# Projection pairs with a fourth PSUM bank, a fixed place for the S5 scan, and weights of merge and output gate cast ahead

## The chip, the cores and the metric

The kernel runs on one core of a Trainium2 chip. The measure is the device time of one execution in microseconds (us). The core has five engines with a queue each: TensorE (PE; matmuls and transposes into PSUM), VectorE (DVE), ScalarE (ACT), GpSimd (POOL) and SyncE (SP, which here only issues DMA transfers). An engine takes its instructions in the order of its queue, so one that waits for a semaphore holds all that stand behind it.

## What is computed

One layer of an encoder: 2048 tokens of width 1024, in float32. The input is normalised, one wide product makes all the projections, four branches (an S5 state-space scan, chunkwise retention, differential attention, cross-attention to 256 memory tokens) are gated each, projected and merged, and one output product is added to the input. Cut to what bears on the change:

```python
h = rms_norm(x, norm_g)
proj = einsum('bsd,dc->bsc', h, w_in)      # 12 pieces of 512 columns, merge: 4 x 1024
ssm_u, ssm_gate, ..., mem_q, mem_gate, merge = split(proj)
# S5: complex diagonal scan over tokens, 32 groups of 16 channels, 64 states each
z = gelu(y + d_skip * u)
a_out = z * sigmoid(z @ w_glu + b_glu) * silu(ssm_gate)      # the output gate (GLU)
branches = stack([a_out, b_out, c_out, m_out])               # S5, retention, differential, memory
br = einsum('bsnc,ncd->bsnd', branches, w_branch)
merged = sum(sigmoid(merge + b_merge) * br, axis=branches)
x = x + merged @ w_out
```

## The kernel before

The tokens are worked in two blocks of 1024 (block 0, block 1). Each block runs through retention, differential attention (with the S5 input u at its tail), **projections** (about 690 to 1183 us in block 0, 2264 to 2750 in block 1), and **merge_output** (to 1460 and 3030), whose output stage ends the block. Every float32 product is made of three passes over operands that are split into a high and a low part: high x high, high x low, low x high. A high part is a cast on ScalarE (names that end in h), a low part the difference, on POOL for weights (L1264 p_l, L460 w1l) and on VectorE for data (br_l, zl, x_t2l). One 128x128 by 128x512 pass is one matmul; twelve of them, four slices of the contraction times three passes, make what is called a product below.

**Projections.** A `Pair` makes 256 columns of w_in for all 1024 tokens by seven products instead of eight (Strassen's scheme): operands t1 to t4 are sums of slices of the activations, mixed on VectorE by `x_mix` at the start, and sums of the weight's quarters a11, a12, a21, a22 are made in `prepare` (L1274 to L1286) from the raw tiles p_r. `product(s)` runs them, in the order 11, t2, t1, t3, 21, 22, t4, into three PSUM banks a, b, c (a from the pool mm, b and c from sc), and `collect(s)` adds what is in a bank to the tiles p_t: L1311 after t2, L1313 and L1314 after t3, L1320 after 22, L1323 after t4. L1314 reads bank c (t1), into which 22 is then written. There are 21 such pairs in a block, behind a first pair that is made in the plain way by `proj_tr`, between the steps of x_mix.

Beside the products, 16 **S5 scans** run in each block (`s5_scan`), one for every eight products: eight small matmuls into a bank of sc (L993), then on VectorE L998 to L1010, one multiply on POOL (L1011), s_x on VectorE (L1014 to L1017), eight more matmuls (L1021, L1023), then a GELU, and z goes to DRAM.

**merge_output.** 32 units (branch n, 128 output columns d), each two times twelve matmuls with a weight of w_branch (w1h, w1l, from a raw tile w_r) and the branch's split output (br_h, br_l), into banks of sc; VectorE multiplies by the gate mg_g (L1238), POOL adds up (L1239). Eight heads and halves of memory attention (`Mem`; m_q, m_kv) are woven into the first 114 of the merge's 128 steps. Then s5b is opened: z is loaded (L1045), split into zh and zl (L1048, L1050), and the **output gate** `s5_glu` runs its products (w_glu, bank mm) between the merge's last steps.

The program is a list of instructions in the order in which the source emits them; a scheduler, at build time, then orders them anew for each engine, so that an instruction may stand ahead of others that come before it in the source. The order of each engine is fixed from then on.

## Time and profile before

| | us |
|---|---|
| three executions, median (lowest, highest) | 3105.1 (3104.0, 3107.03) |
| the profiled execution | 3110.96 |
| its span in the profile | 3109.2 |
| TensorE busy in the span | 2931.0 (94%) |
| VectorE, ScalarE, POOL busy | 1927.7, 1336.3, 1280.6 |

The times in the views are microseconds from the start of the span. A list of waits gives an engine's idle time ahead of a line, by what released it. The chain of waits goes back from the end of a window, at each step to what released it. A window's row gives the busy time and the number of instructions of each engine, and the clock that TensorE was granted, as a share of its higher level.

### The profile page before, as it was taken

What the parts mean: (1) busy time and instruction counts of PE and PEld (TensorE: products, weight loads), DVE (VectorE), ACT (ScalarE), POOL (GpSimd) and SP (SyncE); (2) the same over time, 40 slices, a digit from 0 to 9 for tenths busy, and PEclk for the clock granted to TensorE, in tenths of its full rate; (3) what the DMA queues carried; (4) which work ended last, traced back from release to release, by engine and by line L of the source; (5) the groups of instructions that cost most, each with busy time, mean ns of one, the idle gap of its engine ahead of it and who ended that gap; (6) DMA issues with size and microseconds to landing.
All of it is one profiled execution on the core that took longest, in us unless ns stands there. A gap on an engine that the chain in (4) does not pass through costs nothing.

```text
span 3109.2 us, 43566 instructions
## 1 busy us (share of the span) xinstructions
PE 2931.0 (94%) x14514; PEld 2398.1 (77%) x14514; DVE 1927.7 (62%) x4581; ACT 1336.3 (43%) x3357; POOL 1280.6 (41%) x1189
## 2 busy tenths in 40 slices
PE   5999999998999999989999999999999999999899
PEld 4777777777877877777788878878878878777677
DVE  5885577757655545656543378888776545446654
ACT  3323355553333344423433257776733333344322
POOL 2543543324444543566132242233154444434660
PEclk9999999999999999999999999999999999999999
DMA  5332422133443426555521120121144344355553
GB/s 151 99 90 76 129 72 66 60 91 123 141 137 127 134 102 199 178 179 177 160 73 43 61 64 25 55 60 31 36 139 137 131 138 139 109 175 169 191 159 99
DMA packets 319343, 351.77 MB, mean 113 GB/s; under 512 B 28479, under 2 KB 238478, under 8 KB 319118
## 3 DMA queue, kind: packets, MB, share of 16 engines
q1 hardware_dynamic: 314734, 340.59, 34.9%
q0 software_dynamic: 2304, 8.39, 0.9%
q8 instruction: 115, 1.88, 0.3%
q14 instruction: 110, 0.90, 0.1%
q10 hardware_dynamic: 2080, 0.01, 0.0%
HBM read 247.98 MB, written 100.93 MB: 112 GB/s over the span
## 4 chain that ended last, share of the span: by engine, by line
PE 68%; DVE 12%; POOL 7%; issue 5%; DMA 4%; ACT 3%; SPq 1%; POOLq 0%; DVEq 0%; ACTq 0%
PE sc L1302 17%; PE mm L74 8%; PE mm L76 8%; PE mm L75 8%; PE mm L1302 6%; PE o L806 3%; PE sc L74 3%; PE sc L76 3%; PE sc L75 3%; POOL rms_r L138 2%; PE tr L797 1%; PE sc L752 1%; PE sc L751 1%; POOL mg L1239 1%; DMA w_r<-in_w_in 1%
## 5 line engine op out<-in xcount | busy, mean ns | idle before, releaser
L1264 POOL TENSOR_TENSOR p_l<-p_r,p_h 128x512 fp32r<-128x512 f32 x260 | 364.1, 1402 | 427.8 <-ACT p_h L1263 397.9
L74 PE MATMUL mm<-w5h,xh 128*128 128x512 f32 x1024 | 438.5, 428 | 16.9 <-ACT xh L577 15.6
L75 PE MATMUL mm<-w5l,xh 128*128 128x512 f32 x1024 | 408.2, 399 | 2.9 <-DVE w5l L443 2.9
L76 PE MATMUL mm<-w5h,xl 128*128 128x512 f32 x1024 | 408.9, 399 | 0.0
L138 POOL TENSOR_TENSOR rms_r<-rms_m,mhalf 128x1 f32<-128x1 f32 (+1 forms) x228 | 177.8, 781 | 506.3 <-DVE rms_m L136 437.3
L1263 ACT CAST p_h<-p_r 128x512 fp32r<-128x512 f32 x260 | 160.3, 620 | 345.4 <-DVE p_r L1277 82.5
L758 ACT ACTIVATE pr<-sc,nm 128x512 f32<-128x512 f32 (+3 forms) x320 | 200.1, 626 | 147.0 <-DVE nm L756 145.1
L74 PEld LDWEIGHTS mm<-w5h,xh 128*128 128x128 f32 x1024 | 196.9, 192 | 47.2 <-ACT xh L577 16.0
L76 PEld LDWEIGHTS mm<-w5h,xl 128*128 128x128 f32 x1024 | 195.2, 191 | 44.4
L75 PEld LDWEIGHTS mm<-w5l,xh 128*128 128x128 f32 x1024 | 197.0, 192 | 31.8 <-DVE w5l L443 3.3
L74 PE MATMUL sc<-br_h,w1h 128*128 128x512 f32 x512 | 208.8, 408 | 10.0 <-ACT w1h L459 5.8
L75 PE MATMUL sc<-br_l,w1h 128*128 128x512 f32 x512 | 205.1, 400 | 7.3 <-DVE br_l L1188 7.3
L76 PE MATMUL sc<-br_h,w1l 128*128 128x512 f32 x512 | 205.1, 401 | 0.5 <-POOL w1l L460 0.5
L756 DVE TENSOR_REDUCE nm<-sc 128x1 f32<-128x512 f32 (+3 forms) x320 | 193.3, 605 | 9.1 <-PE sc L752 5.0
L1239 POOL TENSOR_TENSOR mg<-mg,mg_g 128x512 f32<-128x512 f32 x96 | 146.2, 1526 | 96.0 <-DVE mg_g L1238 87.9
L806 PEld LDWEIGHTS o<-vt,at 128*128 128x128 f32 x1088 | 141.8, 192 | 40.5 <-ACT at L799 32.5
L806 PE MATMUL o<-vt,at 128*128 128x128 f32 x1088 | 152.1, 279 | 19.1 <-ACT at L799 18.9
L460 POOL TENSOR_TENSOR w1l<-w_r,w1h 128x512 fp32r<-128x512 f32 x88 | 122.9, 1410 | 98.5 <-ACT w1h L459 89.2
L1302 PE MATMUL sc<-xh,p_h 128*128 128x512 f32 x336 | 138.7, 413 | 22.9 <-DVE p_t L1314 22.3
L443 POOL TENSOR_TENSOR w5l<-w_r,w5h 128x512 fp32r<-128x512 f32 x72 | 97.8, 1360 | 110.2 <-ACT w5h L442 93.3
L1302 PE MATMUL mm<-xh,p_h 128*128 128x512 f32 x336 | 133.4, 397 | 4.4 <-ACT p_t L1309 4.4
L1302 PE MATMUL sc<-xl,p_h 128*128 128x512 f32 x336 | 135.4, 403 | 0.0
(388 smaller groups left out, 7690.5 us busy)
## 6 DMA issues: line engine op xcount, KB each, us to landing
p_r<-in_w_in SPq DMA_DIRECT2D x88, 512.0 KB
w_r<-in_w_in SPq DMA_DIRECT2D x144, 256.0 KB
me_d<-p_t SPq DMA_DIRECT2D x128, 256.0 KB
mg_g<-me_d SPq DMA_DIRECT2D x64, 512.0 KB
s_m<-mats_d SPq DMA_DIRECT2D x32, 640.0 KB
w_r<-br SPq DMA_DIRECT2D x64, 256.0 KB
w_r<-in_w_branch SPq DMA_DIRECT2D x64, 256.0 KB
n_x<-in_x SPq DMA_DIRECT2D x16, 512.0 KB
```

Of the source, the lines that this page charges most:

```text
L74: PE.matmul(out, l[0], r[0], start=first, stop=False)
L75: PE.matmul(out, l[0], r[1], start=False, stop=False)
L76: PE.matmul(out, l[1], r[0], start=False, stop=last)
L138: G.tensor_tensor(r, m, mhalf[:, 0:n], op=ALU.pow)
L460: G.tensor_tensor(lo, raw, hi.bitcast(F32), op=ALU.subtract)
L756: V.tensor_reduce(nm, s[:, 0:n], axis=AX.X, op=ALU.max, negate=True)
L758: A.activation(e[:, 0:n], s[:, 0:n], AF.Exp, bias=nm, accum_out=self.zz[:, m, c:c + 1])
L806: PE.matmul(self.o[:, 0:128], self.at[c][:, q * 128:(q + 1) * 128], self.st["vts"][c][:, q, :], start=c == 0 and q == 0, stop=c * 4 + q == ...
L1239: G.tensor_tensor(dst, dst, t, op=ALU.add)
L1263: A.copy(hi, x)
L1264: G.tensor_tensor(lo, x, hi.bitcast(F32), op=ALU.subtract)
L1302: PE.matmul(o, l[:, k, :], r, start=first and k == 0 and q == 0, stop=k == 3 and q == 2, skip_group_check=True)
```

## The change

- **Pair**: the products come as 11, t2, t1, t3, 21, t4, 22; t4 gets a bank d of its own (pool tr), so that 22 writes bank c one product later. The sums in `collect` follow. The raw tiles p_r come from two pools of two in turn, and the first pair's are loaded in the tail of differential attention.
- **S5 scan**: a scan takes seven products instead of eight, its parts at fixed places behind the products 7j + 1, 7 to 11 and 13; it uses the bank o; the multiply of L1011 goes from POOL to VectorE (32 instructions).
- **Start of the projections**: all four steps of `x_mix` run ahead of each of the first pair's products, and t4 is split ahead of t1.
- **Merge**: the first unit's weight has a pool of its own (w0h, w0l) and is loaded and cast while the last pairs run, with three of the four tiles of the first branch; the rings of w1h and w1l for w_in are four deep instead of six.
- **Output gate**: the split of z is spread in eighths over the merge's steps 4 to 18 behind memory attention, the weights of w_glu are loaded one ahead, and the gate's products begin at step 20 instead of 18.

In the order of the instructions it shows at three places. VectorE, projections of block 0, around the scan whose end stands ahead of L1313 and L1314 (p_t are the collected sums, s_ tiles the scan's, p_s and p_r sums of the weight's quarters). Before:

```order
L1277 TENSOR_TENSOR p_r<-p_s,p_r 128x4x128
L1002 TENSOR_TENSOR s_w<-s_p_11398,s_p_11399 128x128
L1003 TENSOR_TENSOR s_w<-s_p_11398,s_p_11399 128x128
L1007 SCALAR_TENSOR_TENSOR s_y<-rho,carry,s_w 128x128 x2
L1274 TENSOR_TENSOR p_s<-p_r 128x512
L1010 TENSOR_TENSOR s_q_11425<-s_y,s_m 128x256
L1276 TENSOR_TENSOR p_r<-p_r 128x4x128
L1015 TENSOR_TENSOR s_x<-s_q_11425,s_q_11426 128x128
L1016 TENSOR_TENSOR s_x<-s_q_11426,s_q_11425 128x128
L1017 COPY carry<-s_x 128x2
L1313 TENSOR_TENSOR p_t<-sc,p_t 128x512
L1314 TENSOR_TENSOR p_t<-sc,p_t 128x512
```

After, in the middle of block 0 (L1341 to L1353 are the sums, L1304 to L1318 the weights' quarters):

```order
L1011 TENSOR_TENSOR s_q_10917<-s_y,s_m 128x256
L1015 TENSOR_TENSOR s_x<-s_q_10916,s_q_10917 128x128
L1341 TENSOR_TENSOR p_t<-sc,p_t 128x512
L1016 TENSOR_TENSOR s_x<-s_q_10917,s_q_10916 128x128
L1307 TENSOR_TENSOR p_r<-p_s,p_r 128x4x128
L1017 COPY carry<-s_x 128x2
L1304 TENSOR_TENSOR p_s<-p_r 128x512
L1306 TENSOR_TENSOR p_r<-p_r 128x4x128
L1343 TENSOR_TENSOR p_t<-sc,p_t 128x512
L1344 TENSOR_TENSOR p_t<-sc,p_t 128x512
L1014 COPY s_x<-carry 128x2
L1028 SCALAR_TENSOR_TENSOR s_sq<-s_sq,o 128x256
```

The scan's s_x now stands around the sum after t2 (L1341), and the loads' reader L1304 is between it and the sums L1343 and L1344.

ScalarE, start of the merge of block 0 (L1385, after it L1417, are the last pairs' gates; m_qh is the cast of memory attention's query, w1h of a merge weight, br_h of a branch). Before:

```order
L1385 ACTIVATE p_t<-mm,vec 128x512
L1385 ACTIVATE p_t<-p_t,vec 128x512
L1096 CAST m_qh<-m_q 128x512
L459 CAST w1h<-w_r 128x512
L1385 ACTIVATE p_t<-p_t,vec 128x512
L459 CAST w1h<-w_r 128x512
L1098 ACTIVATE m_q<-m_q 128x512
L1096 CAST m_qh<-m_q 128x512
L1098 ACTIVATE m_q<-m_q 128x512
```

After:

```order
L1417 ACTIVATE p_t<-mm,vec 128x512
L1417 ACTIVATE p_t<-p_t,vec 128x512
L459 CAST w1h<-w_r 128x512 x2
L1417 ACTIVATE p_t<-p_t,vec 128x512
L1106 CAST m_qh<-m_q 128x512
L1211 CAST br_h<-w_r 128x512 x2
L1108 ACTIVATE m_q<-m_q 128x512
```

The weights' casts moved ahead of m_qh; the cast of the first branch's last tile, br_h, is behind it (the first weight's, w0h, stands far ahead, among the casts of the last pairs).

VectorE, start of the output gate of block 0 (mg_g is the gated product of a merge unit, zl the low part of z, br_l that of a branch). Before:

```order
L1140 TENSOR_TENSOR m_tl<-tr,m_th 128x512
L1238 SCALAR_TENSOR_TENSOR mg_g<-mg_g,sc 128x512 x4
L1050 SCALAR_TENSOR_TENSOR zl<-z_st,zh 128x128 x16
L1238 SCALAR_TENSOR_TENSOR mg_g<-mg_g,sc 128x512
L1050 SCALAR_TENSOR_TENSOR zl<-z_st,zh 128x128 x16
L1188 TENSOR_TENSOR br_l<-w_r,br_h 128x512 x4
L1238 SCALAR_TENSOR_TENSOR mg_g<-mg_g,sc 128x512 x4
L1070 SCALAR_TENSOR_TENSOR g_t<-g_t,z_st 128x512
```

After:

```order
L1265 SCALAR_TENSOR_TENSOR mg_g<-mg_g,sc 128x512 x4
L1055 SCALAR_TENSOR_TENSOR zl<-z_st,zh 128x128 x9
L1265 SCALAR_TENSOR_TENSOR mg_g<-mg_g,sc 128x512
L1055 SCALAR_TENSOR_TENSOR zl<-z_st,zh 128x128 x11
L1265 SCALAR_TENSOR_TENSOR mg_g<-mg_g,sc 128x512
L1055 SCALAR_TENSOR_TENSOR zl<-z_st,zh 128x128 x3
L1212 TENSOR_TENSOR br_l<-w_r,br_h 128x512 x4
L1265 SCALAR_TENSOR_TENSOR mg_g<-mg_g,sc 128x512
L1055 SCALAR_TENSOR_TENSOR zl<-z_st,zh 128x128 x6
L1265 SCALAR_TENSOR_TENSOR mg_g<-mg_g,sc 128x512
```

Ahead of br_l there are 23 pieces of zl instead of 32, and one gated product more.

The diff, cut to its core:

```diff
     def w_in128(p, c):
-        return [load_w128(p, w_in[i * 512:(i + 1) * 512, c:c + 128]) for i in range(2)]
+        return [load_w128(p, w_in[i * 512:(i + 1) * 512, c:c + 128], bufs=4) for i in range(2)]
...
         fm, em0, em1, dm, tb = [mt[:, i, :].rearrange("p (r c) -> p r c", r=2) for i in range(5)]
-        v = ps_sc()
+        v = ps_o()
         for g2 in range(2):
...
         V.tensor_tensor(q1, y, cosb, op=ALU.mult)
-        G.tensor_tensor(q2, y, sinb, op=ALU.mult)
+        V.tensor_tensor(q2, y, sinb, op=ALU.mult)
...
             zs.append(st)
+        return zs, zh, zl
+
+    def s5_zsplit(z):
+        zs, zh, zl = z
+        for k, st in enumerate(zs):
             hv = zh[:, k, :].rearrange("p (c s) -> p s c", s=8)
             A.mul(hv, st, 0.5)
             for s in range(8):
                 V.scalar_tensor_tensor(zl[:, k, :].rearrange("p (c s) -> p s c", s=8)[:, s, :], st[:, s, :], 0.5,
                                        hv[:, s, :].bitcast(F32), op0=ALU.mult, op1=ALU.subtract)
-        return zs, zh, zl
-
-    def s5_glu(b, e, w1, p, z):
+                if s % 4 == 3:
+                    yield
+
+    def s5_wg(w1, e):
+        return load_w128(w1, a["ssm_w_glu"][0][:, e * 128:(e + 1) * 128]) if e < 4 else None
+
+    def s5_glu(b, e, w1, p, z, ws):
         zs, zh, zl = z
-        wg = load_w128(w1, a["ssm_w_glu"][0][:, e * 128:(e + 1) * 128])
+        wg = ws.pop(e)
+        ws[e + 1] = s5_wg(w1, e + 1)
         for hf in range(2):
...
 
         def prefetch(self):
             self.pools.append(self.cx.enter_context(pool("mrga", side="right")))
+            self.w0 = self.cx.enter_context(pool("w0", side="right"))
+            self.raw = self.raw_w(0)
+
+        def raw_w(self, u):
+            n, d = self.units[u]
+            return raw_w128(a["w_branch"][0][n][:, d * 128:(d + 1) * 128])
+
+        def first(self):
+
+            hi, lo = [self.w0.tile([128, 4, 128], F32R, name=n) for n in ("w0h", "w0l")]
+            A.copy(hi, self.raw)
+            G.tensor_tensor(lo, self.raw, hi.bitcast(F32), op=ALU.subtract)
+            self.wb[0] = hi, lo
+            self.raw = self.raw_w(1)
...
         def open(self):
             cx = self.cx
             self.gx = ExitStack()
-            self.raw = raw_w128(a["w_branch"][0][self.units[0][0]][:, 0:128])
             self.pools.append(cx.enter_context(pool("mrgb", side="right")))
             self.w1 = cx.enter_context(pool("w128m", side="right"))
             mp = cx.enter_context(pool("merged", side="right"))
             self.gp = self.gx.enter_context(pool("gates", side="right"))
-            self.fetch(0, self.raw)
             self.load(2, 3)
+            self.gate(0)
             self.merged = [mp.tile([128, TB], F32, name=f"mg{k}") for k in range(8)]
 
-        def fetch(self, u, raw=None):
-
+        def fetch(self, u):
+
+            if u < len(self.units):
+                self.wb[u] = load_w128(self.w1, None, self.raw if u == 1 else self.raw_w(u))
+                self.gate(u)
+
+        def gate(self, u):
             if u < len(self.units):
                 n, d = self.units[u]
-                self.wb[u] = load_w128(self.w1, a["w_branch"][0][n][:, d * 128:(d + 1) * 128], raw)
                 t = self.gp.tile([128, TB], F32, name="mg_g", bufs=3)
...
-        def __init__(self, b, c, sink, xs, pw, pe):
-            self.c, self.sink, self.xs, self.pw, self.pe, self.w = c, sink, xs, pw, pe, {}
-            self.ps = {}
+        def __init__(self, c, pr):
+            self.c, self.pr, self.w, self.ps = c, pr, {}, {}
+
+        def bind(self, sink, xs, pw, pe):
+            self.sink, self.xs, self.pw, self.pe = sink, xs, pw, pe
+            return self
 
         def load(self):
             self.raw = []
             for kh in range(2):
-                r = self.pw.tile([128, 4, 2, 128], F32, name="p_r", bufs=4)
+                r = self.pr.tile([128, 4, 2, 128], F32, name="p_r", bufs=2)
                 DMA.dma_start(out=r, in_=w_in[kh * 512:(kh + 1) * 512, self.c:self.c + 256].rearrange(
                     "(k p) (i c) -> p k i c", p=128, i=2))
                 self.raw.append(r)
...
             elif s == 4:
                 self.w[4] = self.split(a12)
             elif s == 5:
+                self.w[5] = self.split(a22)
+            else:
                 V.tensor_tensor(a12, a12, a11, op=ALU.subtract)
-                self.w[5] = self.split(a12)
-            else:
-                self.w[6] = self.split(a22)
+                self.w[6] = self.split(a12)
 
         def product(self, s):
-            x = self.xs[("11", "t2", "t1", "t3", "21", "22", "t4")[s]]
-            bank = "abcbacb"[s]
-            if s < 3:
-                self.ps[bank] = ps_mm() if s == 0 else ps_sc()
+            x = self.xs[("11", "t2", "t1", "t3", "21", "t4", "22")[s]]
+            bank = "abcbadc"[s]
+            first = s < 3 or s == 5
+            if first:
+                self.ps[bank] = ps_mm() if s == 0 else ps_tr() if s == 5 else ps_sc()
             o = self.ps[bank]
             wh, wl = self.w.pop(s)
-            first, last = s < 3, True
             for k in range(4):
                 xh, xl = x[0][:, k, :], x[1][:, k, :]
                 for q, (l, r) in enumerate(((wh, xh), (wh, xl), (wl, xh))):
...
                               skip_group_check=True)
 
         def collect(self, s):
-            pa, pb, pc = [self.ps.get(q) for q in "abc"]
+            pa, pb, pc, pd = [self.ps.get(q) for q in "abcd"]
             if s == 0:
                 self.t = [self.pe.tile([128, 512], F32, name="p_t", bufs=7) for _ in range(3)]
                 A.copy(self.t[0], pa)
...
                 V.tensor_tensor(self.t[1], pb, self.t[0], op=ALU.add)
             elif s == 3:
                 V.tensor_tensor(self.t[2], pb, self.t[0], op=ALU.add)
-                V.tensor_tensor(self.t[2], pc, self.t[2], op=ALU.add)
-                self.sink(1, 1, self.t[2], self.t[2])
+                V.tensor_tensor(self.t[0], pc, self.t[2], op=ALU.add)
+                self.sink(1, 1, self.t[0], self.t[0])
             elif s == 4:
                 t = self.pe.tile([128, 512], F32, name="p_t", bufs=7)
                 self.sink(0, 0, pa, t)
             elif s == 5:
+                V.tensor_tensor(self.t[2], pd, self.t[2], op=ALU.add)
+                self.sink(1, 0, self.t[2], self.t[2])
+            elif s == 6:
                 V.tensor_tensor(self.t[1], pc, self.t[1], op=ALU.add)
                 self.sink(0, 1, self.t[1], self.t[1])
-            elif s == 6:
-                V.tensor_tensor(self.t[0], pb, self.t[0], op=ALU.add)
-                self.sink(1, 0, self.t[0], self.t[0])
 
     def x_mix(b, k, xs, xm):
...
         split(t2, xs["t2"])
         yield
-        split(t1, xs["t1"])
-        yield
         split(b12, xs["t3"])
         yield
         t4 = raw(x0h, x0l, 4 + k, "x_c", 2)
...
         V.tensor_tensor(t4, t4, xs["t2"][1][:, k, :].bitcast(F32), op=ALU.subtract)
         split(t4, xs["t4"])
         yield
-
-    def projections(b, mg):
+        split(t1, xs["t1"])
+        yield
...
             with pool("xm", side="right") as xm:
-                raw = []
-                first = pair(MQ_C, keep(q_d[b][0:2]))
-                first.load()
+                for u, x in enumerate(pairs):
+                    x.pr = (pw, first.pr)[u % 2]
                 pairs[0].load()
                 ws = [[first.split(first.raw[kh][:, :, i, :]) for kh in range(2)] for i in range(2)]
                 mixes = [x_mix(b, k, xs, xm) for k in range(4)]
-                for i in range(2):
-                    for hf in range(2):
-                        next(mixes[2 * i + hf])
-                        o = ps_mm()
-                        drain(proj_tr(o, b, hf, ws[i]))
-                        t = pe.tile([128, 512], F32, name="p_t", bufs=7)
-                        first.sink(i, hf, o, t)
-                for q in range(3):
-                    if q == 1:
+                for q, (i, hf) in enumerate(((0, 1), (1, 1), (0, 0), (1, 0))):
+                    for x in mixes:
+                        next(x)
+                    if q == 2:
                         for g in range(LEAD):
                             prepare(g)
-                    for x in mixes:
-                        next(x)
+                    o = ps_mm()
+                    drain(proj_tr(o, b, hf, ws[i]))
+                    t = pe.tile([128, 512], F32, name="p_t", bufs=7)
+                    first.sink(i, hf, o, t)
             sx = ExitStack()
             sp = sx.enter_context(pool("s5a", side="right"))
             side = {}
...
 
             for j in range(NPAIR):
                 gen = scan(j)
-                for q, at in enumerate((-6, 1, 2, 3, 5, 6, 7)):
-                    side.setdefault(max(8 * j + at, 0), []).append(gen)
+                for at in (1, 7, 8, 9, 10, 11, 13):
+                    side.setdefault(7 * j + at, []).append(gen)
+            n = len(steps)
             for g, (u, s) in enumerate(steps):
                 prepare(g + LEAD)
                 pairs[u].product(s)
                 pairs[u].collect(s)
                 for gen in side.get(g, []):
                     next(gen)
-                if g == len(steps) - 17:
+                if g == n - 24:
                     sx.close()
+                    ux.close()
                     mg.prefetch()
-                if g in (len(steps) - 13, len(steps) - 9, len(steps) - 5):
-                    mg.load(2, (g - len(steps) + 13) // 4)
+                if n - 24 <= g < n - 6 and (n - g) % 6 == 0:
+                    mg.load(2, (g - n + 24) // 6)
+                if g == n - 7:
+                    mg.first()
 
...
             events.run()
         with pool("s5b") as sp:
             z = s5_z(b, sp)
-            glus = chain_of(s5_glu(b, e, mg.w1, sp, z) for e in range(4))
-            for q in range(128 - MEM_STEPS):
+            zsplit = s5_zsplit(z)
+            ws = {}
+            glus = chain_of(s5_glu(b, e, mg.w1, sp, z, ws) for e in range(4))
+            for q in range(128 - MEM_STEPS + 64):
                 next(merge)
-            for q in range(64):
-                next(merge)
-                if q >= 4:
+                if q == 12:
+                    ws[0] = s5_wg(mg.w1, 0)
+                if 4 <= q < 20 and q % 2 == 0:
+                    next(zsplit)
+                if q >= 20:
                     next(glus, None)
             drain(glus)
...
-        w1 = []
+        ahead = []
 
         def tail():
-            w1.append(w1x.enter_context(pool("w128")))
+            pr = prx.enter_context(pool("praw"))
+            w1 = w1x.enter_context(pool("w128"))
+            ahead.append(Pair(MQ_C, pr))
             with pool("us") as up:
                 for e in range(4):
-                    yield from s5_input(b, e, w1[0], up)
+                    if e == 3:
+                        ahead[0].load()
+                    yield from s5_input(b, e, w1, up)
 
         dense = diff_branch(b, wp, wx.close, tail)
         drain(dense)
```

## Rows read from the trace of the kernel before

**Rows 1.** The page, part 1: busy time of each engine, share, instructions.
```profile
PE 2931.0 (94%) x14514; PEld 2398.1 (77%) x14514; DVE 1927.7 (62%) x4581; ACT 1336.3 (43%) x3357; POOL 1280.6 (41%) x1189
```
**Rows 2.** Waits of PE, 690 to 1183: waited for, us, times, longest.
```profile
PE sc L1302 <- DVE p_t L1314: 11.0, 6, 2.9
PE sc L1302 <- DVE p_t L1313: 4.1, 1, 4.1
PE mm L1302 <- ACT p_t L1309: 2.2, 1, 2.2
```
**Rows 3.** Waits of PE, 2264 to 2750.
```profile
PE sc L1302 <- DVE p_t L1314: 11.3, 6, 2.5
PE sc L1302 <- DVE p_t L1311: 3.2, 1, 3.2
```
**Rows 4.** Waits of PE, 1183 to 1345.
```profile
PE mm L74 <- ACT w1h L459: 4.8, 1, 4.8
PE sc L75 <- DVE br_l L1188: 3.7, 1, 3.7
PE sc L74 <- ACT w1h L459: 2.5, 1, 2.5
```
**Rows 5.** Waits of PE, 2750 to 2915.
```profile
PE mm L74 <- ACT w1h L459: 4.4, 1, 4.4
...
PE sc L74 <- ACT w1h L459: 3.3, 1, 3.3
```
**Rows 6.** The chain of waits, 1095 to 1116: start, us, what.
```profile
1096.56 2.72 PE mm L1302 x12
...
1109.24 0.98 POOL s_q L1011
...
1111.51 0.28 DVE s_x L1016
...
1112.47 0.66 DVE p_t L1314
```
**Rows 7.** The chain of waits, 1170 to 1200.
```profile
1178.75 5.50 DMA m_q<-q_d
```
**Rows 8.** The chain of waits, 1300 to 1345.
```profile
1317.99 8.45 POOL mg L1239
...
1328.37 5.93 DMA w_r<-in_w_branch
```
**Rows 9.** Windows: length, busy of PE, PEld, DVE, ACT, POOL; PE's clock; DMA.
```profile
940.60:944.00 3.40, 3.40 (x10) 2.61 (x9) 0.00 (x0) 0.98 (x3) 1.28 (x1) 0.50 0.40 154
2705.30:2708.70 3.40, 3.40 (x8) 2.72 (x9) 0.00 (x0) 1.76 (x3) 1.28 (x1) 0.50 0.62 219
1183.00:1193.00 10.00, 7.09 (x28) 5.61 (x29) 2.60 (x5) 4.97 (x9) 2.54 (x3) 0.83 1.03 351
2751.00:2761.00 10.00, 7.00 (x18) 5.28 (x19) 2.11 (x3) 4.97 (x9) 2.51 (x2) 0.66 0.98 318
722.00:740.00 18.00, 11.73 (x38) 8.38 (x37) 14.18 (x20) 6.07 (x11) 11.64 (x5) 0.79 0.52 175
2290.00:2316.00 26.00, 19.95 (x88) 15.09 (x87) 18.51 (x33) 7.06 (x13) 16.20 (x9) 0.87 0.42 147
1312.00:1322.70 10.70, 7.43 (x32) 5.51 (x30) 10.68 (x33) 7.99 (x7) 4.71 (x1) 1.00 0.34 136
1322.70:1333.00 10.30, 5.76 (x12) 3.58 (x12) 4.38 (x8) 0.47 (x1) 6.19 (x3) 0.67 0.51 154
1333.00:1343.00 10.00, 8.06 (x24) 6.02 (x25) 1.31 (x2) 3.82 (x7) 7.49 (x7) 0.66 0.60 182
```
**Rows 10.** DVE by line, 860 to 1060: xcount, busy, mean ns, idle before.
```profile
L1015 DVE TENSOR_TENSOR s_x<-s_q,s_q 128x128 f32<-128x128 f32 x9 | 8.0, 894 | 5.1 <-POOL s_q L1011 5.1
...
L1010 DVE TENSOR_TENSOR s_q<-s_y,s_m 128x256 f32<-128x256 f32 x9 | 3.8, 424 | 0.3
```
**Rows 11.** Waits of DVE, 690 to 1183.
```profile
DVE p_s L1274 <- DMA p_r<-in_w_in: 11.2, 12, 1.9
```

21 lines of the change are left out of this document (13 added, 8 removed).

## Prediction

> **What bounds the kernel now.** I read the page first: TensorE is busy for 2931.0 of 3109.2 us, 94% [rows 1]. No other engine comes near, and the change leaves the number of matmuls alone, so all that can be won lies in the 178 us in which TensorE stands, and in the time in which it runs at the lower of its two clock levels. Next I read TensorE's waits in the two stretches of the projections [rows 2, 3] and around the two starts of merge and output gate [rows 4, 5]. Then I followed the chain of waits through one wait of each kind [rows 6 to 8] to see what was late, and last the clock in the windows behind these waits [rows 9]. The reader should see four kinds of wait that the change reaches: a steady one (bank c, released by L1314), one at the start of the projections, one at the start of the merge, and two close together at the start of the output gate.
>
> **The clock is part of each price.** Behind a wait the granted clock is halved for a while: 0.50 (1.2 instead of 2.4 GHz) in the windows at 940.6 and 2705.3 [rows 9], where a 3.4 us window does 1.7 us of work. Seven of the twelve steady waits are followed by such a stretch (these two windows are the first and the last); the shorter ones are not. In a longer window the loss is its length times (1 minus clock).
>
> **Steady wait: minus 34 us.** In the chain of rows 6 the scan's vector work stands in VectorE's queue ahead of L1313 and L1314: the POOL multiply of L1011 (0.98 us), then s_x, then L1314 (0.66 us), after which the product "22" may write bank c. Only one product, "21", covers this; one costs 2.72 us [rows 6], and the tail of the scan alone, from L1011 to the end of L1314, takes 3.9 us there. So TensorE stands: 11.0 us in block 0 and 11.3 us in block 1, six times each [rows 2, 3]. Now "t4" has a bank of its own and goes ahead of "22", and the scan has one fixed place in each run of seven: its first matmuls behind "11", its vector work under "t2", "t1", "t3" (3 x 2.72 = 8.2 us), its second matmuls behind these. The order shows it: L1344 is no longer directly behind s_x, and between "t3" and "22" there are two products, 5.4 us, instead of one. I estimate from the vector rows that s_x is ready about 2 us before it is wanted and L1344 done about 4 us before. Moving L1011's multiply to VectorE costs 32 instructions of 0.42 us there (its twin L1010 in rows 10), 14 us on an engine with slack, and saves its hand-over: L1015 takes 0.89 us on average [rows 10], against 0.28 us of an undisturbed s_x in rows 6, because it meets POOL. Gain: 22.3 us of waiting, and 7 x 1.7 = 11.9 us of clock, together 34. Bounds: 26, if a quarter of the waits stays near the ends of the blocks, where weights and branch outputs are now loaded in between; 36, with small waits on s_x gone too.
>
> **Start of the projections: minus 2 (block 0) and minus 5 (block 1).** In block 0 TensorE waits 2.2 us for L1309 and 4.1 us for L1313, in block 1 3.2 us for L1311 and again 2.2 us in a row that reads like block 0's [rows 2, 3], and the windows there lose 18.0 x 0.21 = 3.8 and 26.0 x 0.13 = 3.4 us of clock [rows 9]. All of it would be 10 and 9 us. But the cause is VectorE's long run of operand mixing, under which POOL's casts of the weights starve, and the run is as long as before. The raw weights of the first pair are loaded ahead, yet POOL's first low part still waits for the mixing to pause. By the order L1307, which makes the second product's weight, now stands behind all four splits of t4, and the cast that reads it behind the copy of the first product. So in block 0 a wait of about 4 us, at half clock behind it, appears at the second product; I take 2 us of the 10, with minus 3 (a loss) to 4 as bounds. Block 1 has its loads earlier; I expect one wait of 1 to 3 us and one slow stretch to stay: 9 less 4 is 5, bounds 3 to 9.
>
> **Start of the merge: minus 2.5 and minus 4.** TensorE waits 2.5 us and 3.3 us for the cast of the first merge weight [rows 4, 5]. It was queued on ScalarE behind the cast of m_q, whose load takes 5.50 us [rows 7]; the windows lose 10.0 x 0.17 = 1.7 and 10.0 x 0.34 = 3.4 us of clock [rows 9]. Whole price: 4.2 and 6.7. Now w0 is cast before the last pairs end, and 18 matmuls (4.1 us) need nothing else, then six of the second unit (1.4 us). But by the order the cast of br_h of the fourth block stands behind that same m_q cast, and m_q is loaded later than before, behind two gate loads and a store of the last pair. If it lands 4 to 6 us after the last product, br_h is ready after 5 to 7 us and its low part after 7: TensorE stands 0 to 2.5 us there. I take 2.5 and 4; bounds 0 to 4.2 and 1 to 6.7.
>
> **Start of the output gate: minus 6.5 in each block.** Before, TensorE waits 3.7 us for br_l (block 1's row reads the same), and soon after 4.8 us (4.4 in block 1) for the GLU weight [rows 4, 5]; the two windows lose 10.3 x 0.33 and 10.0 x 0.34, 6.8 us of clock [rows 9]. The name "split ahead" promises all of it, some 15 us a block. The order doesn't give that: the loads of z still stand behind the last store of memory attention, so the split starts when it did, and the weight is loaded into a raw buffer that br_l has to free. What changes is this. VectorE's 33 operations between 1312.0 and 1322.7 took 10.68 us, 0.32 each [rows 9]; ahead of the first br_l there are now 23 pieces of zl and two gate products instead of 32 and one. That is 9 x 0.32, less 0.6 for a gate product: br_l comes 2.2 us sooner, and the wait falls to 1.5 us, which I expect to leave the clock high. The weight's load was held on SP's queue behind a gate load that waited for POOL's L1239, 8.45 us long [rows 8], as it could not finish while VectorE ran back to back. That run ends 2.2 us sooner, and the GLU weight is now first instead of second in line (0.9 us); the load takes 5.93 us [rows 8] as before. So the first gate matmul starts 3.1 us sooner, and the second slow stretch stays: 3.1 plus 3.4 of clock, 6.5. Bounds: 3 (both slow stretches stay) and 15 (POOL gets its turn between the split's parts, and the weight is there). At this place rule and row part. The trace shows POOL losing to a run of some 20 VectorE instructions. The Trainium skill, "SBUF — State Buffer", section "Who interferes with whom", has a pair of ports taken for one whole instruction by whichever side starts first, which would let POOL in behind the first of them. By that rule the SP queue would be free early and the weight bound by br_l alone; that would be worth about 2 us more in each block, a sum of 64 instead of 60. The row decides for me.
>
> **Sum.** 34 + 2 + 5 + 2.5 + 4 + 13 = 60.5 us, from the profiled execution's 3110.96 to 3050.5. That execution lies 5.9 us above the median of the three runs, 3105.1; I take the same difference off the median: 3044.6. Of the loads moved ahead, the first pair's two, the first merge weight's and three of branch outputs now stand in SP's queue in the tail of differential attention, among the stores of u. Their issue and landing I cost at nothing: the first reader of u is the first scan, behind the first pair, and if that cover were gone, the scan would wait for u and show it in its first matmuls alone. Nothing else should move: the order is the same up to the end of block 0's differential attention, and the output stage isn't touched.
>
> **The rivals.** (A) The steady waits go, but each start only exchanges its wait: the mixing holds L1307 instead of L1313, m_q holds br_h instead of the weight, z is as late as it was. Then only 26 to 36 us and a few at the gate remain: 3063 to 3079. For it speaks that in each of the three places the same late thing is still in the queue; against it, that the covers have grown by 2 to 5 us. Chance 0.21. (B) The starts are really hidden: 34, 8 and 9, 4 and 7, 15 and 15, together about 92: 3005 to 3025. For it: less POOL work and shorter VectorE runs; against it: the loads of z and m_q are no earlier. Chance 0.14. (C) Slower: VectorE becomes what TensorE waits for. L1304 waits for the load of a pair's raw weights, 11.2 us in 12 times in block 0 before [rows 11], and now stands in VectorE's queue directly ahead of L1343 and L1344, in every pair. The slack there is 4 us; a load that is 6 us late holds "22" by 2 us and costs 1.7 us of clock, in each of 42 pairs: 155 us lost against 60 gained, about 3200. It decides from a load 4 us late, or an average loss of 1.4 us a pair. The raw buffers are still four, the longest such wait was 1.9 us, so 0.05. (D) The change does nothing: only if the bank were not what "22" waits for; the chain names it, so 0.03, at 3105.
>
> **How the numbers follow.** My forecast case, 3025 to 3063, has 0.57. The range must leave out no more than 0.2: from 3012 (most of B) to 3080 (A). A measurement of this kernel can tell about 0.2%, 6 us, from no change. Faster than 3099: forecast, A, B, 0.92. Same 0.03, slower 0.05.
>
> **What would show it.** In the profile after: no row of TensorE waiting for the eviction into bank c (L1343, L1344) above 2 us in sum; s_x ready before the scan's second matmuls; a wait of about 4 us at block 0's second product, released by ScalarE or POOL; at the merge, waits for br_h or br_l of 0 to 2.5 us in place of the weight; at the gate, br_l about 1.5 us and the weight 3 to 5 us. I am wrong if "PE waits for VectorE" grows in the steady pairs (C), or if the gate's weight is no longer in the list of waits (B).

## The result and the profile after

| | median of 4, us | lowest to highest |
|---|---|---|
| before | 3104.55 | 3099.8 to 3107.03 |
| after | 3053.53 | 3045.78 to 3058.4 |

The ratio is 0.9831, 95% interval 0.9814 to 0.9848: faster by 51 us. The profiled execution took 3045.78 us, the shortest of the four; its first Strassen product starts at 709.42 us instead of 717.13. The plain first pair ahead of it takes as long as before (26.80 us, before 26.74), so these 7.7 us lie ahead of the projections, where only a few loads were added. In the profiles of the changed kernel and of the twelve kernels below, the plain pair starts anywhere from 682.6 to 688.3 us, before at 690.4. I take the 7.7 us for spread between executions, and compare the lengths of stages and not the spans.

The engines' busy times after (part 1 of the page, against [rows 1]):

```profile
PE 2899.1 (95%) x14514; PEld 2381.9 (78%) x14514; DVE 1920.5 (63%) x4613; ACT 1332.3 (44%) x3357; POOL 1247.0 (41%) x1157
```

The matmuls are the same 14514, but take 31.9 us less: that is clock, granted at 0.98 on average before and at 0.99 after. Windows cut at the first products of each part (the merge's at the end of the last projection product) show where the time went. In each kernel the rows are, for block 0 and then for block 1: first Strassen pair, 20 further pairs, merge up to the gate's first product, gate up to the output stage. Columns: stretch, length, busy of PE, PEld, DVE, ACT and POOL with counts, PE's clock, DMA share, GB/s. Before:

```profile
717.13:751.25 34.12, 27.48 (x110) 20.95 (x109) 24.70 (x39) 8.36 (x15) 18.13 (x10) 0.85 0.35 115
751.25:1182.98 431.73, 420.71 (x1978) 342.35 (x1976) 224.86 (x393) 160.09 (x272) 194.44 (x152) 0.99 0.39 128
1182.98:1334.10 151.12, 136.93 (x675) 111.13 (x675) 95.35 (x196) 69.84 (x146) 72.90 (x52) 0.96 0.61 196
1334.10:1445.12 111.02, 108.45 (x462) 87.96 (x462) 61.94 (x72) 28.20 (x59) 73.85 (x54) 0.97 0.57 172
2286.14:2316.17 30.03, 23.98 (x105) 18.43 (x104) 22.48 (x39) 10.19 (x20) 17.33 (x9) 0.89 0.37 128
2316.17:2750.69 434.52, 423.21 (x1981) 344.37 (x1979) 223.85 (x390) 159.67 (x270) 194.45 (x152) 0.98 0.39 127
2750.69:2903.74 153.05, 137.89 (x677) 112.02 (x676) 94.72 (x196) 69.60 (x146) 73.15 (x52) 0.95 0.60 192
2903.74:3015.01 111.27, 108.69 (x462) 88.12 (x462) 61.73 (x72) 28.21 (x59) 73.13 (x54) 0.97 0.56 173
```

After:

```profile
709.42:737.23 27.81, 21.73 (x86) 17.14 (x85) 19.03 (x26) 9.01 (x16) 16.07 (x11) 0.88 0.39 133
737.23:1153.95 416.72, 416.72 (x2002) 342.45 (x2001) 223.53 (x420) 160.19 (x275) 185.24 (x138) 1.00 0.41 134
1153.95:1295.17 141.22, 134.06 (x679) 110.18 (x677) 96.04 (x194) 68.18 (x143) 67.91 (x51) 0.99 0.65 205
1295.17:1410.41 115.24, 108.50 (x461) 87.69 (x459) 63.83 (x75) 28.00 (x59) 74.03 (x55) 0.97 0.55 170
2250.05:2276.59 26.54, 23.16 (x85) 17.39 (x85) 17.98 (x23) 7.81 (x14) 14.69 (x10) 0.87 0.42 149
2276.59:2693.19 416.60, 416.60 (x2002) 342.56 (x2001) 223.03 (x419) 160.48 (x275) 185.30 (x138) 1.00 0.41 133
2693.19:2837.15 143.96, 134.89 (x678) 110.95 (x677) 96.92 (x195) 68.11 (x144) 68.63 (x52) 0.98 0.62 202
2837.15:2949.37 112.22, 107.53 (x461) 87.03 (x460) 61.44 (x74) 27.88 (x59) 73.27 (x54) 0.98 0.57 174
```

Read these rows twice: length less PE busy is the time in which TensorE stands (is idle); PE busy at equal work shows the clock. In the 20 pairs TensorE stood 11.0 and 11.3 us before and stands 0.0 and 0.0 after, at clock 1.00. The first pair's window and that of the others must be added up, since the scan's new places move 20 to 24 matmuls from the first window into the second. Together, the **projections** of both blocks went from 930.4 to 887.7 us: 25.6 less of standing, 17.2 less of clock, **42.7**. **Merge and gate** went from 526.5 to 512.6: 6.8 of standing, 7.0 of clock, **13.8**. That is 56.5 in these two executions; the medians differ by 51, which the spread of some 10 us between executions covers.

The plain first pair has one wait in block 0 after, 3.3 us for POOL's p_l, where it had 2.1 and 0.7 us before. TensorE's waits behind it, at the start of the projections (690 to 737); from 737 to 1154 the list is empty, where [rows 2] had six waits for L1314:

```profile
PE sc L1332 <- ACT p_h L1293: 3.6, 1, 3.6
PE sc L1332 <- POOL p_l L1294: 2.5, 1, 2.5
```

In the merge and at the gate's start, 1154 to 1307, against [rows 4]:

```profile
PE sc L75 <- DVE br_l L1212: 3.4, 1, 3.4
PE mm L76 <- POOL w1l L460: 1.3, 1, 1.3
...
PE sc L74 <- ACT br_h L1211: 0.9, 1, 0.9
```

The waits for w1h, 2.5 and 4.8 us, are gone; br_l still waits. The list of the whole span has a row which is new:

```profile
PE mm L74 <- ACT g_t L1077: 6.4, 2, 3.7
```

These are 3.7 us in block 0 and 2.7 in block 1, behind the gate's start, where the gate's tanh is late and keeps its bank. That is most of the 4.2 us by which the gate's stretch in block 0 got longer. The chain of waits in block 1 (start, us, what) shows how it comes about:

```profile
2869.09 1.29 POOL w1l L460
2870.38 2.12 POOL mg L1266
2872.52 0.32 SPq L1236
2872.95 0.37 SPq L1210
2873.41 4.96 DMA w_r<-in_w_branch
...
2878.99 0.69 ACT g_t L1077
2879.73 0.50 PE mm L74
```

POOL's addition stands behind a weight's low part; SP's load of the next gate tile (L1236) waits for that addition, and the loads of a branch output (L1210) and of a weight, whose casts stand ahead of the tanh on ScalarE, stand behind it.

### The profile page after: what moved, and what is told of

The parts are those of the page before. It is cut to its first block, busy times and chain, and to the rows that moved or that the text cites. A ratio compares the mean times of both kernels' runs of the same rounds, so it can differ in the third digit from the quotient of the medians.

```text
span 3043.5 us, 43500 instructions
## 1 busy us (share of the span) xinstructions
PE 2899.1 (95%) x14514; PEld 2381.9 (78%) x14514; DVE 1920.5 (63%) x4613; ACT 1332.3 (44%) x3357; POOL 1247.0 (41%) x1157
## 5 line engine op out<-in xcount | busy, mean ns | idle before, releaser
L1294 POOL TENSOR_TENSOR p_l<-p_r,p_h 128x512 fp32r<-128x512 f32 x260 | 368.4, 1420 | 458.3 <-ACT p_h L1293 445.3
L75 PE MATMUL sc<-br_l,w1h 128*128 128x512 f32 x496 | 197.3, 398 | 6.9 <-DVE br_l L1212 6.9
L74 PE MATMUL sc<-br_h,w1h 128*128 128x512 f32 x496 | 200.5, 404 | 3.3 <-DVE mg_g L1265 3.3
L76 PE MATMUL sc<-br_h,w1l 128*128 128x512 f32 x496 | 197.3, 398 | 0.0
L1332 PE MATMUL sc<-xh,p_h 128*128 128x512 f32 x336 | 131.3, 391 | 0.6 <-ACT p_h L1293 0.6
```

The costliest lines, as they stand in the source:

```text
L74: PE.matmul(out, l[0], r[0], start=first, stop=False)
L75: PE.matmul(out, l[0], r[1], start=False, stop=False)
L76: PE.matmul(out, l[1], r[0], start=False, stop=last)
L1294: G.tensor_tensor(lo, x, hi.bitcast(F32), op=ALU.subtract)
L1332: PE.matmul(o, l[:, k, :], r, start=first and k == 0 and q == 0, stop=k == 3 and q == 2, skip_group_check=True)
```

## The experiments

Each kernel was run beside the kernel before on one chip. "Projections" and "merge and gate" are the sums of the four windows each, as above, from its profiled execution.

| edit, against the changed kernel | median, us | ratio to before (interval) | projections | merge and gate |
|---|---|---|---|---|
| none (e1) | 3050.68 | 0.983 (0.9809, 0.9851) | 888.4 | 515.2 |
| banks of before (e2) | 3057.28 | 0.9843 (0.9822, 0.9865) | 894.4 | 513.1 |
| scan's places of before (e3) | 3051.14 | 0.9833 (0.9811, 0.9854) | 890.6 | 510.9 |
| both (e4) | 3081.29 | 0.9929 (0.9904, 0.9955) | 917.8 | 512.3 |
| both, multiply on POOL (e11) | 3093.38 | 0.9956 (0.9942, 0.9969) | 929.2 | 515.3 |
| first weights prepared a step earlier (e8) | 3050.12 | 0.9827 (0.9812, 0.9842) | 887.7 | 516.5 |
| merge weight of before (e12) | 3051.87 | 0.9827 (0.9813, 0.984) | 888.1 | 511.9 |
| gate of before (e5) | 3055.64 | 0.9844 (0.9828, 0.986) | 888.1 | 519.3 |
| four gate tiles (e6) | 3051.89 | 0.9833 (0.9819, 0.9848) | 889.2 | 515.7 |
| gate weights not ahead (e9) | 3053.89 | 0.9832 (0.9819, 0.9846) | 888.4 | 515.0 |
| z split in wider pieces (e7) | 3047.63 | 0.982 (0.9804, 0.9837) | 888.1 | 505.9 |
| e7 and e9 (e10) | 3047.08 | 0.9807 (0.9794, 0.9821) | 889.7 | 508.3 |

The seven kernels whose merge and gate are the changed one's (after, e1 to e4, e8, e11) show how far that column is to be trusted: mean 513.7, from 510.9 to 516.5 (e3, e4 and e11 load the merge's first tiles some products later).

**Once more (e1).** The changed kernel as it is.

> The changed kernel as it is, as the reference for the runs beside it. Expected: 3040 to 3062 us, ratio to before about 0.983; in the profile the twenty steady pairs of block 0, from the second pair's first product to the last product's end, again 416 to 418 us (before: 431.7).

Measured: 3050.68 us, and the same list of waits, with 3.4 us on g_t in block 0. The new wait is no accident of one execution.

**Fourth bank or scan's place (e2, e3, e4).** e2 puts back the order and the banks:

```diff
-            x = self.xs[("11", "t2", "t1", "t3", "21", "t4", "22")[s]]
-            bank = "abcbadc"[s]
+            x = self.xs[("11", "t2", "t1", "t3", "21", "22", "t4")[s]]
+            bank = "abcbacb"[s]
```

e3 puts back the scan's places (and the loads of the merge's first tiles, which are set by the same count); e4 does both.

```diff
-                for at in (1, 7, 8, 9, 10, 11, 13):
-                    side.setdefault(7 * j + at, []).append(gen)
+                for at in (-6, 1, 2, 3, 5, 6, 7):
+                    side.setdefault(max(8 * j + at, 0), []).append(gen)
```

> The changed kernel with the banks and the product order of before (22 ahead of t4, three banks), the scan in its new fixed place. Theory: what 22 waits for is the scan's vector work queued between t3's end and L1344; with the scan in step that work is done under t2, t1 and t3, so one product of cover (2.7 us against 1.4 us for two sums) is enough, and the gain stays: steady pairs of block 0 at 416 to 420 us, the total within 5 us of the changed kernel. Rival (the bank is the cause, whatever the scan does): steady pairs back at 428 to 432 us, the total about 30 us slower than the changed kernel.

> The changed kernel with the scan's places of before (every eight products, parts spread at -6, 1, 2, 3, 5, 6, 7; the merge's tiles loaded six products later, since the scans end later), the fourth bank kept. Theory (cover): the waits of before were 1.1 to 2.9 us, and the fourth bank adds a product of 2.7 us between the sum and the product that needs it, so nearly all of the steady gain stays: steady pairs at 416 to 421 us. Rival (the scan's place is what counts): the scan's vector work delays other sums as well, for instance its own second matmuls, which wait on s_x under one product: steady pairs at 425 to 432 us.

> Both undone: banks and product order of before, and the scan's places of before. Both theories expect the steady waits back: steady pairs of block 0 at 428 to 433 us, the total 25 to 35 us slower than the changed kernel (about 3080). If it stays near 417 us, neither edit carries the gain, and it would be the multiply that went to VectorE, or the bank of the scan.

Waits for L1344 in the further pairs of block 0, e2 and then e4 (e3 has none):

```profile
PE sc L1332 <- DVE p_t L1344: 1.7, 1, 1.7
```

```profile
PE sc L1332 <- DVE p_t L1344: 9.0, 4, 2.5
```

Either edit alone keeps nearly all of the gain (e2 loses 6.7 us in the projections, e3 2.9), and only without both do the waits return: 30 us in the projections, 28 to 31 in the medians. The two are not two gains but two covers for the wait that the prediction named: the scan's tail must not end directly ahead of the eviction, or the eviction must have two products of time. But e4's projections are still 12.6 us shorter than before, which neither explains.

**The multiply (e11).** As e4, and L1011 back on POOL:

```diff
-        V.tensor_tensor(q2, y, sinb, op=ALU.mult)
+        G.tensor_tensor(q2, y, sinb, op=ALU.mult)
```

> Edit: the products' order, their three banks and the scan's places as before the change, and with them the scan's last multiply back on POOL; merge, gate and start of the projections as changed. With banks and scan undone but the multiply still on VectorE the 20 steady pairs of a block took 426.0 us, against 431.7 and 434.5 in the kernel before and 416.7 in the changed one. Theory (the rest of the steady gain is that multiply: it takes the hand-over from POOL, about 1 us, out of each scan's tail, which stands straight ahead of L1344): the pairs take 430 to 435 us, waits of the tensor engine on VectorE's additions into the third bank are 10 to 13 us a block, as before; total 10 to 15 us above the run with banks and scan undone, about 3090 to 3097. Rival (the rest comes from the casts' order or from spread between executions): the pairs stay at 425 to 427 us and the total at about 3081.

Waits in the further pairs of block 0, to be held against e4's row above:

```profile
PE sc L1332 <- DVE p_t L1344: 12.6, 6, 2.9
```

L1015, which makes s_x from the two multiplies, in e4 and then e11 (lowest, median and highest duration, ns):

```profile
L1015 DVE TENSOR_TENSOR s_x<-s_q,s_q x32: 276/294/1376, 737.0 to 2657.7; 128x128 f32<-128x128 f32 x32
```

```profile
L1015 DVE TENSOR_TENSOR s_x<-s_q,s_q x32: 294/1350/1432, 737.4 to 2670.4; 128x128 f32<-128x128 f32 x32
```

The theory held: the 20 pairs take 433.9 and 432.4 us, in e4 426.0 and 426.1; the projections are 11.4 us longer, the medians 12.1 us apart (8 by the ratios, whose intervals still overlap). More than a hand-over is behind it. With the multiply on POOL, L1015 is released as POOL goes on to its next instruction, and takes 1350 ns instead of 294; in the kernel before, behind the multiply of [rows 6], POOL starts a weight's low part at 1110.17, and L1015, from 1110.24, takes 1.35 us.

The projections of e11 are 1.2 us from before's. So all but a microsecond of the 42.7 is in these three edits together; the new order at the start, the scan's bank o and the two pools of raw tiles, which this kernel still has, give nothing that can be measured without them. What the multiply is worth where the cover is there was not tried.

**Start of the projections (e8).** The weights of the first pair's products are prepared one step of the mixing earlier:

```diff
-                    if q == 2:
+                    if q == 1:
```

> The changed kernel with the first four weights of the second pair prepared one product earlier, so that L1307 stands ahead of the four splits of t4 on VectorE. Theory: the waits of 3.6 us (ScalarE's cast) and 2.5 us (POOL's) at block 0's second product come from L1307 behind these splits; they go, and from the first Strassen product to the second pair block 0 falls from 28.3 to 22 to 25 us; the total 3 to 8 us faster. Rival: the work is only exchanged, t4's splits or the third product's x_t1 are late instead, with a wait of 3 to 6 us in the same stretch, and the total stays within 3 us.

The waits of 700 to 740:

```profile
PE sc L1332 <- POOL p_l L1294: 5.6, 1, 5.6
```

POOL's first low part there (start, us, line):

```profile
709.69 10.62 POOL L1294 TENSOR_TENSOR p_l<-p_r,p_h 128x512 fp32r<-128x512 f32 x1 [16.06 <-ACT p_h L1293]
```

The theory fell and the rival held: from the first Strassen product to the second pair it takes 27.4 us (27.8 in the changed kernel, 28.3 in e1). The wait for ScalarE's p_h turned into one for POOL's p_l, 5.6 us instead of 3.6 and 2.5: the low part, where the next one takes 1.27 us, takes 10.62 under VectorE's mixing and ends behind it. The place is held by POOL under the mixing, as in the prediction.

**Merge weight (e12).** The first weight is loaded and split when the merge starts:

```diff
...
-                if g == n - 7:
-                    mg.first()
```

> Edit: the merge's first weight is loaded and split when the merge starts, as before the change; all else as changed. Theory (the merge's start gave 2.5 and 4 us): the wait for that weight at the first merge product is back, 2 to 3.5 us in each block, with a stretch at the lower clock behind it, the wait for br_h there (0.9 and 1.6 us) is gone; total 5 to 9 us above the changed kernel. Rival (only exchanged: the load of m_q is late anyway and the merge's later products wait for it): the stretch from the last projection to the gate's first product stays within 1.5 us of 141 and 144 us; total within 3 us.

TensorE's waits from 1150 to 1180, and ScalarE's instructions from 1155 to 1163 (start, us, line):

```profile
PE sc L74 <- ACT br_h L1209: 1.6, 1, 1.6
PE sc L74 <- ACT w1h L459: 0.5, 1, 0.5
```

```profile
1156.23 1.14 ACT L459 CAST w1h<-w_r 128x512 fp32r<-128x512 f32 x2 [1.10 <-PE sc L1333]
...
1162.14 0.62 ACT L1106 CAST m_qh<-m_q 128x512 fp32r<-128x512 f32 x1 [4.15 <-DMA m_q<-q_d]
```

The theory fell: w1h comes 0.5 us late, not 2 to 3.5, and merge and gate are as short as with the weight ahead. The edit gives up the early load and cast, but the cast still stands ahead of m_qh, which comes 5.8 us after the last projection product; before, it was queued behind m_qh [rows 7]. So I read that its place in the queue counts, and not the head start; no run puts the cast back behind m_qh.

**Gate (e5).** Split of z in one piece, no weight ahead, gate products from step 18:

```diff
...
-                if 4 <= q < 20 and q % 2 == 0:
-                    next(zsplit)
-                if q >= 20:
+                if q >= 18:
```

> The changed kernel with the output gate of before: z split in one go, the gate's weights not loaded ahead, its products from step 18 on. Theory: the gate's part of the change won some 5 us a block up to the gate's first product (from the last pair's end 141.4 us in block 0; expected 146 to 148 us here, with a wait of 3.5 us for br_l and one of 4 to 5 us for the weight), and lost some of it behind, in a new wait for g_t (from the gate's first product to the output stage 113.5 to 115.2 us; expected back at 110 to 112 us). Total 2 to 8 us slower than the changed kernel. Rival: the merge's early weight alone gave the gain in this stretch; then the first number stays at 141 to 143 us and the total is the same or lower.

Waits from 1154 to 1315:

```profile
PE mm L74 <- ACT w1h L459: 4.9, 1, 4.9
PE sc L75 <- DVE br_l L1209: 3.7, 1, 3.7
```

The theory held: both waits of [rows 4] at the gate are back, and the wait for g_t is gone from both blocks. Merge and gate take 519.3 us against the mean of 513.7: the gate's edit is worth 5.6 us in all, with 2.8 and 8.4 against the ends of that column.

**What makes the tanh late (e6, e9).** e6 gives the gate tiles a fourth buffer; e9 splits only the first gate weight ahead.

```diff
-                t = self.gp.tile([128, TB], F32, name="mg_g", bufs=3)
+                t = self.gp.tile([128, TB], F32, name="mg_g", bufs=4)
```

```diff
-        wg = ws.pop(e)
-        ws[e + 1] = s5_wg(w1, e + 1)
+        wg = ws.pop(0) if e == 0 else s5_wg(w1, e)
```

> The changed kernel with four buffers instead of three for the gate tiles mg_g. Theory: the new wait of 3.4 to 3.7 us for g_t in block 0 (2.7 in block 1) comes from the SP queue: a gate tile's load waits there for POOL's addition, and the load of a branch tile behind it comes late, holds its cast on ScalarE and, behind that, the tanh that frees the gate's bank. With one more buffer the gate load waits for an addition one half-unit earlier: the wait for g_t falls below 1 us, from the gate's first product to the output stage 109 to 111 us, the total 4 to 12 us faster than the changed kernel. Rival (the branch tile's own transfer is late, or ScalarE is just full): no change, 113 to 115 us.

> Edit: in the output gate only the first column's GLU weight is split ahead of its turn; each later one is loaded and split when its column is entered, as before the change. The split of the first weight ahead of the merge's end stays. Theory (the new wait behind the gate's start has its cause in the weights that are split one column ahead: POOL stands on a low part for which the ring of split weights has no free buffer, behind it POOL's gated product, behind that the load of the next gate tile and the load of the branch output on SP's queue, behind that ScalarE's cast and then its tanh, whose bank the tensor engine waits for): the wait on ScalarE's tanh (3.7 and 2.7 us in the profile after) falls below 1 us, and the stretch from the gate's first product to the output stage goes back from 112 to 115 us to 110 to 112, with no weight wait over 2 us in its place; total 2 to 4 us below the changed kernel. Rival (the late tanh comes from the later loads of the branch output alone, whatever the weights do): the tanh wait stays within 1 us of what it was. Second rival (only exchanged): the tanh wait goes, and a wait of 2 to 5 us for the second column's weight comes in its place; total unchanged.

Waits of 1290 to 1420 in e6, then of 1310 to 1420 in e9:

```profile
PE mm L74 <- ACT g_t L1077: 5.9, 2, 3.2
```

```profile
PE mm L74 <- ACT g_t L1076: 3.4, 1, 3.4
```

Both theories fell: neither edit takes the wait away (3.4 and 2.0 us in e1). That POOL's addition holds SP's queue is not refuted by it: with a fourth gate tile the gate tiles' loads still wait 10.2 us for that addition from 1318 to 1350, in the changed kernel 12.5, in e5 5.7. ScalarE in e9, 1331 to 1348, shows the tanh (L1076) behind the cast of the branch output, as in the changed kernel:

```profile
1345.01 0.62 ACT L1210 CAST br_h<-w_r 128x512 fp32r<-128x512 f32 x1 [7.81 <-DMA w_r<-br]
...
1346.43 0.68 ACT L1076 ACTIVATE g_t<-mm,vec 128x512 f32<-128x512 f32 x1
```

The branch output is the gate's own, stored and read back. In e5 its load stands ahead of the gate tile's on SP's queue at this place, in the changed kernel, e7 and e9 behind it. I take it that the gate's start at step 20 instead of 18 brings this order about; that is argued, and was not tried.

**Wider pieces (e7, e10).** zl is made in eight instructions instead of 32; e10 joins it with e9's edit.

```diff
-            for s in range(8):
-                V.scalar_tensor_tensor(zl[:, k, :].rearrange("p (c s) -> p s c", s=8)[:, s, :], st[:, s, :], 0.5,
+            for s in range(0, 8, 4):
+                V.scalar_tensor_tensor(zl[:, k, :].rearrange("p (c s) -> p s c", s=8)[:, s:s + 4, :], st[:, s:s + 4, :], 0.5,
```

> The changed kernel with the low part of z made by eight instructions of 128x4x128 instead of 32 of 128x128. Theory: br_l is late because 23 short zl instructions at 0.32 us stand ahead of it on VectorE (7.4 us), stretched by POOL's addition to up to 1.5 us each; an instruction of 512 elements takes about 0.7 us as the others of that size do, so seven of them take 4 to 5 us, br_l comes 2 to 3 us sooner and its wait of 3.4 us falls to 0 to 1.5 us; the total 3 to 9 us faster. Rival: the wait is set by the loads of z and the casts on ScalarE (2.2 us each), not by VectorE: no change of more than 1 us at that wait.

> The edit of the experiment with four blocks in one vector instruction in the low split of z, and that with the gate's later weights not split ahead, together, as the version that may beat both. Theory (the tanh wait hangs on the weight ring, the br_l wait on ScalarE's casts of z): br_l wait stays at 3 to 4 us in each block, the tanh wait is under 1 us, the gate from its first product to the output stage takes 108 to 111 us; total 3 to 6 us below the changed kernel, and within 2 us of the wide split alone, since both take away the same wait. Rival (the two gains are of different kinds and add up): 6 to 9 us below.

Waits of e7 from 1154 to 1307 and from 1307 to 1415, and what ScalarE and then VectorE did ahead of br_l (1274 to 1296):

```profile
PE sc L75 <- DVE br_l L1211: 3.9, 1, 3.9
```

```profile
PE mm L74 <- ACT g_t L1076: 1.5, 1, 1.5
```

```profile
1279.19 8.33 ACT L1053 ACTIVATE zh<-z_st 128x1024 fp32r<-128x1024 f32 x4 [8.19 <-DMA z_st<-z_d]
```

```profile
1281.40 3.40 DVE L1055 SCALAR_TENSOR_TENSOR zl<-z_st,zh 128x512 fp32r<-128x512 f32 x3 [2.06 <-ACT zh L1053]
...
1289.06 1.56 DVE L1055 SCALAR_TENSOR_TENSOR zl<-z_st,zh 128x512 fp32r<-128x512 f32 x1
1290.55 3.56 DVE L1211 TENSOR_TENSOR br_l<-w_r,br_h 128x512 fp32r<-128x512 f32 x4
```

The wait for br_l didn't move, but not because of ScalarE, as the rival has it: its casts of z end at 1287.52, and VectorE, without a gap from 1281.40 on, comes to br_l at 1290.55. From the first zl to there it takes 9.15 us, 1.0 less than in the changed kernel (10.18). POOL's second addition beside it takes that back: the four br_l take 3.56 us instead of 2.48, the first of them 1.75 instead of 0.68, so that it is ready 10.9 us after the first zl in both. Yet merge and gate, 505.9 us, lie below all seven of the column above; the wait for g_t fell from 3.7 and 2.7 to 1.5 and 1.2 us, for a reason that stays open. e10 is no better than e7, and its waits for g_t, 2.7 and 1.6 us, are above the 1 us expected: the weight ring is not their cause. At 3047 both are some 3 to 6 us below the changed kernel's two medians and beat both kernels on the medians, but the intervals of the ratios overlap; that they are faster than the changed kernel is likely, not shown.

## Why the prediction was right, point by point

The forecast was 3045 us, in a range from 3012 to 3080; the median is 3053.5. The sum was 60.5 us, the stages gave 56.5, the medians 51.

- **Steady waits and start of the projections, 34 + 7 = 41 predicted, 42.7 measured.** The 22.3 us of steady waiting went to zero, as the step says. More came back from the clock than I had counted from the seven slow stretches, and less from the start, where TensorE still stands 6.1 of 6.6 us in block 0 and 3.4 of 6.1 in block 1. By standing and granted clock of the first pair's windows I estimate some 5 us for the start and 38 for the pairs; that the sum comes within 2 us is in part luck, the more so as e11, which keeps the start's edits, has only 1.2 us left of the 42.7. The wait at block 0's second product is there, released by ScalarE and POOL as predicted; 6.1 us, not 4; block 1 keeps one wait, 2.6 us for xl, inside the 1 to 3 predicted. What I mis-stated is the worth of one part: I described the multiply's move as a saved hand-over within the 34, and with the old rotation it alone is worth 8 to 12 (e11 against e4). And I had the fourth bank and the scan's place as acting together, where either alone is enough (e2, e3).
- **Merge and gate, 6.5 + 13 = 19.5 predicted, 13.8 measured.** This is the term that was mis-sized. The merge's part came, with waits for br_h of 0.9 and 1.6 us, inside the 0 to 2.5 predicted; by difference it is some 7 us. Its reason was half right: the early load and cast didn't matter (e12), the order on ScalarE's queue is what is left.
- **The gate, 13 predicted, 5.6 measured (e5).** Both numbers within the step were off, in opposite directions. br_l was to wait 1.5 us and waits 3.4 and 3.6. I had VectorE come to br_l 2.2 us sooner, by nine pieces of zl less and one gated product more; from the first zl it takes 10.18 us instead of 10.76, only 0.6 less, because POOL's second addition now runs beside the last three pieces, which take 2.62 us where three others take 1.0. The weight was to wait 3 to 5 us and waits 1.3 and 0.4: its load took 2.9 us (issued at 1290.19, cast at 1293.1) instead of the 5.93 that I carried over from [rows 8]. That row is a merge weight's load; the gate weight's own, among two gate tiles and two merge weights, took 5.6 (issued at 1327.83, cast at 1333.43). Then 3.7 and 2.7 us of a new wait for the tanh took part of it back; I had stopped at the gate's first product and not followed the queue of SP beyond it.
- **POOL's addition.** This is where rule and row parted. POOL (1276 to 1297) and then VectorE (1276 to 1292) around the split of z, after:

```profile
1283.02 6.00 POOL L1266 TENSOR_TENSOR mg<-mg,mg_g 128x512 f32<-128x512 f32 x2 [3.75 <-DVE mg_g L1265]
```

```profile
1279.31 3.04 DVE L1055 SCALAR_TENSOR_TENSOR zl<-z_st,zh 128x128 fp32r<-128x128 f32 x9 [1.41 <-ACT zh L1053]
...
1282.79 3.71 DVE L1055 SCALAR_TENSOR_TENSOR zl<-z_st,zh 128x128 fp32r<-128x128 f32 x11
1286.35 0.75 DVE L1265 SCALAR_TENSOR_TENSOR mg_g<-mg_g,sc 128x512 f32<-128x512 f32 x1
1286.94 2.62 DVE L1055 SCALAR_TENSOR_TENSOR zl<-z_st,zh 128x128 fp32r<-128x128 f32 x3
1289.49 2.48 DVE L1212 TENSOR_TENSOR br_l<-w_r,br_h 128x512 fp32r<-128x512 f32 x4
```

  Two additions take 6.0 us where one took 8.45 [rows 8], the first of them 4.63. While the eleven pieces run at 0.34 us each, POOL doesn't finish; it ends at 1287.65, 1.30 us after the start of L1265, which reads PSUM, and an undisturbed addition takes 1.29. So the run, and not one instruction of it, held POOL, as the row had said. The second addition starts beside pieces of zl, and there the pieces wait: three take 2.62 us. By the rule of the Trainium skill, "SBUF — State Buffer", section "Who interferes with whom", that the side which starts first has the pair of ports for one whole instruction, I had POOL get in behind the first piece; at the first addition the trace doesn't agree, at the second it does. What I had named as that rule's consequence came about in both blocks all the same, by the gated product between the pieces: SP was free at 1287.67, and the weight's load went out at 1290.19, when the first br_l had freed its buffer (1290.17).
- **Rivals.** A (each start only exchanges its wait) holds for the start of the projections in block 0 and for br_l, not for the merge and the weight. B came true for the gate's weight alone, of which 1.3 and 0.4 us are left, and the tanh took that back. C has nothing in the trace: no wait for L1343 or L1344 remains, so the loads under L1304 were never late enough: VectorE waits 3.2 us for them there in block 0, three times, instead of 11.2. Everything costed at nothing in the tail of differential attention shows no wait there either.

## What to carry to other kernels

Where a wait has two possible covers, ask what each does alone before adding them up: here either of them took all but 3 to 7 of 30 us. Carry a transfer's duration over only with the traffic that stood around it, and follow a moved step past its first consumer, down each queue, until the next read-back of its result. Before a cast is moved far ahead, look at what stands ahead of it in its queue: here it was enough that what came late no longer did. And an instruction handed to a second engine costs more than its hand-over when that engine's next instruction slows the one that waited for it.

## What the runs showed that was not expected

- One multiply of 128x256 moved from POOL to VectorE, 16 times a block, gave 8 to 12 us in all in the kernel with the old banks and places, although POOL was busy only 41% of the span: on POOL it made the scan's tail longer directly ahead of an eviction on which TensorE waits, by a slower L1015 above all.
- The clock's part of the gain in the projections (17.2 us) was two thirds of that of the waits themselves (25.6). A few waits more or fewer can decide it: the 20 pairs of block 0 in e4, with 9.0 us of waits for L1344, take 417.1 us of PE busy at 1.00, in e11, with 12.6, 421.3 at 0.99, for the same 1982 matmuls.
- Pieces of zl four times as wide, with a strided output, gain little by the element: three of 128x512 took 3.40 us in e7, where nine of 128x128 took 3.04 in the changed kernel, which is 1.13 against 4 x 0.34 = 1.35 us.
